# DA q and k projected feature-major, rotary rows exchanged by DMA, attention steps at a priority lifted by 300 places

## The chip, the cores and the metric

One core of a Trainium2 chip runs the program. The metric is the device time of one execution in microseconds (us), as the median of several executions. Five engines take instructions in order, each from its own queue: TensorE (PE, matmuls into PSUM, with weight loads shown apart as PEld), VectorE (DVE), ScalarE (ACT), GpSimd (POOL) and SyncE (SP, which here issues DMAs only). They wait for each other through semaphores.

## The reference, cut to what matters

Two layers of a hybrid mixer run on 512 tokens `x` of width 1024, with 256 context tokens `ctx` that only layer 0 updates. Each layer projects the tokens, runs differential attention (DA, 4 heads), grouped-query attention (GQA, 8 heads on 2 key heads) and a Hyena long convolution, and projects the three outputs back.

```python
h = _rms(x, norm_g[l]) * (1.0 + scale[:, None]) + shift[:, None]
qa, ka, va, ga, qg, kg, vg, gg, uh, gh = _prep(h @ w_in[l], gq_q_g[l], gq_k_g[l])
...
ka_all = jnp.concatenate([ka_c, _rope_2d(ka, tab_da)], axis=1)
va_all = jnp.concatenate([va_c, va], axis=1)
...
y = _mixer_output(_rope_2d(qa, tab_da), ka_all, va_all, ga, _rope_2d(qg, tab_gq), kg_all, vg_all, gg,
                  uh, gh, filt, ...)

def _rope_1d(x, cos, sin):
    x1, x2 = jnp.split(x.astype(jnp.float32), 2, axis=-1)
    return jnp.concatenate([x1 * cos - x2 * sin, x2 * cos + x1 * sin], axis=-1)

def _diff_attend(q, k, v, lam):   # per block of 128 queries
        s = jnp.einsum('bqhcd,bkhcd->bhcqk', qb, k).astype(jnp.float32) * scale
        p = jax.nn.softmax(s, axis=-1)
        a = (p[:, :, 0] - lam * p[:, :, 1]).astype(v.dtype)
        return jnp.einsum('bhqk,bkhe->bqhe', a, v)
```

A DA head has two components c, each with 64 features for q and for k. The rotary step mixes, within a component, feature d with feature d+32 of the same token.

## The kernel before

Every fp32 product is made of three fp32r matmuls (`mm3`, L138 to L140) from a high part and a low part of both factors. The normalized tokens lie in SBUF with features on the partitions (`hT`, as `hx` and `hc`). There are two ways to project. `proj_tok` takes a pair of 128-token blocks as the stationary factor and 256 weight columns as the moving one: tokens come out on the partitions of a PSUM tile `pst` (2 x 8 x 3 = 48 matmuls of 256 columns). `proj_feat` takes 128 weight columns as the stationary factor and all 512 tokens as the moving one: features come out on the partitions of `psf` (8 x 3 = 24 matmuls of 512 columns). Both share two PSUM buffers (`pj`).

The loop over the DA heads works like this before. For each of two pairs of token blocks, `proj_tok` gives q and k of one head token-major. DVE multiplies by the cosine table (L1039) and, with the halves of each component exchanged, by the sine table (L1043, two instructions); POOL adds or subtracts the two (L1046, two instructions). Four PE transposes (L1050) bring the result back into the same PSUM tile, features on partitions. `evac_q` and `evac_k` split it from there into the high and low tiles of pool `up` (20 buffers), with the two components in separate slots. There are 4 heads in each of 2 layers, 8 of these blocks in all; the context's q and k come from `proj_feat` without a rotary step.

Attention is written as generators. `da_att` makes for each group j of 256 queries the scores (`scores_c`, tile S), the softmax (max on DVE, exponential on ACT), the combination of the two components, and then `pv`: for each group of 256 keys four PE transposes of the probabilities (L648, tile T), the split into ph (ACT, L581) and pl (DVE, L582), and the products with V into O (L655 to L658). T and O have one PSUM buffer each. The generators stand in the queue `att`, and each projection calls `att.tock()`, which lets an attention step in at a set pace, so that the steps of one head lie among the projections of the next.

That is the order in which the program is traced. A scheduler then lays each engine's instructions out by priority, which is the place in that traced order, so what stands beside what on an engine is decided when the program is built. SP's queue carries the weight loads (`raw`, `adaw`), the gates (`gl`) and the attention results (`yx`).

Of the kernel before, what the change touches and what calls it, by code (L numbers as in the profile page):

```python
# [3 lines left out]

# [6 lines left out]
F32 = mybir.dt.float32  # L11
F32R = mybir.dt.float32r
AF = mybir.ActivationFunctionType
# [21 lines left out]
class Background:  # L35


    def __init__(self):
        self.queue = deque()
        self.pace = self.due = 1.0  # L40

    def add(self, gen):
        self.queue.append(gen)
# [11 lines left out]
    def tick(self):  # L55
        while self.queue:
            try:
                next(self.queue[0])
                return
            except StopIteration:  # L60
                self.queue.popleft()
# [7 lines left out]
def hybrid_mixer(ctx: ExitStack, tc: tile.TileContext, a, out):  # L69
    nc = tc.nc  # L70
# [49 lines left out]

    bg = Background()
    slow = Background()
    att = Background()
    pre = Background()

    def col(l, c, n=1):
# [407 lines left out]
    def layer(l, hx, hc, late, first):  # L534
# [87 lines left out]
        def scores_c(c, q, kT, klist, i):  # L622
            S = pS.tile([128, 1024], F32, tag="S", name="S")
            m = slice(i * 128, (i + 1) * 128)
            for n, kp in enumerate(klist):
                kh, kl = kT[kp]
                ps = S[:, n * 256:(n + 1) * 256]
                PE.matmul(ps, q[:, c, m], kh[:, c], start=True, stop=False)
                PE.matmul(ps, q[:, c, m], kl[:, c], start=False, stop=True)
            return S  # L630

        def softmax(S, n):
# [359 lines left out]
        for pr in range(2):  # L992
            W = wchunk(l, DA_C[pr]["v"])
            V = {}
            for p in pairs:
                ps = proj_tok(W, p)
                vh = up.tile([128, 2, 256], F32R, tag="u", name="vh")
                vl = up.tile([128, 2, 256], F32R, tag="u", name="vl")
                evac_split(vh, vl, ps)
                V[p] = (vh, vl)  # L1000
            if pr == 0:
                gates(wchunk(l, DA_C[0]["gate"]), 8)
            for hh in range(2):
                head = 2 * pr + hh
                if head == 1:
                    gates(wchunk(l, DA_C[1]["gate"]), 10)
                W = wchunk(l, DA_C[pr]["qk"][hh])
                qT, kT = {}, {}

                def evac_q(p, ps):  # L1010
                    st = up.tile([128, 2, 256], F32R, tag="u", name="qT")
                    ACT.activation(st, ps.unsqueeze(1).to_broadcast([128, 2, 256]), AF.Copy, scale=0.125)
                    for c in range(2):
                        r, o = slice(64 * c, 64 * c + 64), slice(64 - 64 * c, 128 - 64 * c)
                        DVE.scalar_tensor_tensor(out=st[o, c], in0=ps[r], scalar=0.125, in1=st[r, c].bitcast(F32),
                                                 op0=ALU.mult, op1=ALU.subtract)
                    qT[p] = st

                def evac_k(p, ps):
                    kh = up.tile([128, 2, 256], F32R, tag="u", name="kH")  # L1020
                    kl = up.tile([128, 2, 256], F32R, tag="u", name="kL")
                    for c in range(2):
                        POOL.memset(kl[64 - 64 * c:128 - 64 * c, c].bitcast(F32), 0.0)
                    ACT.activation(kh, ps.unsqueeze(1).to_broadcast([128, 2, 256]), AF.Copy)
                    for c in range(2):
                        r = slice(64 * c, 64 * c + 64)
# [3 lines left out]
                    kT[p] = (kh, kl)  # L1030

                for p in (0, 1):
                    ps = proj_tok(W, p)
                    v = ps.rearrange("p t (c d) -> p t c d", d=64)
                    t1 = tp.tile([128, 2, 4, 64], F32, tag="tp", name="t1")
                    t2 = tp.tile([128, 2, 4, 64], F32, tag="tp", name="t2")
                    cb = cosD[:, 2 * p:2 * p + 2].unsqueeze(2).to_broadcast([128, 2, 8, 32])
                    sb = sinD[:, 2 * p:2 * p + 2].unsqueeze(2).to_broadcast([128, 2, 4, 32])
                    DVE.tensor_tensor(out=t1.rearrange("p t c (h d) -> p t (c h) d", d=32),  # L1039
                                      in0=ps.rearrange("p t (c d) -> p t c d", d=32), in1=cb, op=ALU.mult)  # L1040
                    for h in range(2):
                        d, o = slice(32 * h, 32 * h + 32), slice(32 - 32 * h, 64 - 32 * h)
                        DVE.tensor_tensor(out=t2[:, :, :, d], in0=v[:, :, :, o], in1=sb, op=ALU.mult)  # L1043
                    for h in range(2):
                        d = slice(32 * h, 32 * h + 32)
                        POOL.tensor_tensor(out=t1[:, :, :, d], in0=t1[:, :, :, d], in1=t2[:, :, :, d],  # L1046
                                           op=ALU.add if h else ALU.subtract)
                    for qk in range(2):
                        for t in range(2):
                            PE.transpose(ps[:, qk, t * 128:(t + 1) * 128],  # L1050
                                         t1[:, t, 2 * qk:2 * qk + 2].rearrange("p c d -> p (c d)"), ident)
                    evac_q(p, ps[:, 0])
                    evac_k(p, ps[:, 1])
                if full:
                    evac_q(2, proj_feat(W, 0, False))
                evac_k(2, proj_feat(W, 1, False))
# [295 lines left out]
    sinD = cp.tile([128, 4, 32], F32, tag="sinD", name="sinD")  # L1352
    SP.dma_start(sinD, a["sinD"])

    bg.add(f0)
# [6 lines left out]
def _constants():  # L1362
# [19 lines left out]
        return f(np.cos(ang)), f(np.sin(ang))  # L1382

    c["cosG"], c["sinG"] = axial(128)
    c["cosD"], c["sinD"] = axial(64)
# [113 lines left out]
```

## Time and profile before

| | before |
|---|---|
| median of 3 runs | 1597.02 us (1595.21 to 1600.0) |
| profiled execution, its own time | 1593.43 us |
| its span | 1591.7 us |
| granted TensorE clock, share of full | 0.989 |
| PE busy | 1510.1 us, 95% |
| DVE busy | 1127.6 us, 71% |
| ACT busy | 830.9 us, 52% |
| POOL busy | 415.6 us, 26% |

The span runs from the first to the last instruction of the profiled execution. Its own time is 1.7 us longer than the span, and the median of the runs stands 3.6 us above that execution. A matmul's busy time overlaps the next one's, so what a matmul costs on PE is the distance between the starts of two neighbours in the timeline.

### The profile page before, as it was taken

The numbers are of one execution on the slowest core, as the hardware profiler recorded it, in microseconds if no ns is written. First come the engines' busy times: TensorE is split into PE (matmuls) and PEld (weight loads), VectorE is DVE, ScalarE is ACT, GpSimd is POOL, SyncE is SP. The second block draws the span as 40 slices with busy tenths as digits, with TensorE's granted clock in tenths as the row PEclk, the third lists the DMA queues.
The fourth block names the chain that finished last, engine by engine and source line by source line (L and its number), as shares of the span: only waits on it lengthen the run. The fifth ranks groups of instructions, "written<-read, shape, count | busy, mean of one in ns | idle before, by whom it ended". The sixth has DMA issues, their size and how long they took to land.

```text
span 1591.7 us, 29098 instructions
## 1 busy us (share of the span) xinstructions
PE 1510.1 (95%) x11126; PEld 1398.6 (88%) x11126; DVE 1127.6 (71%) x2222; ACT 830.9 (52%) x1673; POOL 415.6 (26%) x451
## 2 busy tenths in 40 slices
PE   5989999999999999998999999999999999898997
PEld 3768889999898989798999977888999998898997
DVE  6789667877776475777755378869877756768755
ACT  5645243555556555566653256334546556656643
POOL 0243443212212141113002114334222222214032
PEclk9999999999999999999999999999999999999999
DMA  9437676423435253315352334674422232115441
GB/s 344 145 111 263 192 222 200 129 76 96 143 102 169 93 159 117 113 48 195 117 179 94 93 108 145 213 229 146 152 75 87 87 97 87 57 51 182 130 133 70
DMA packets 105952, 216.87 MB, mean 136 GB/s; under 512 B 11345, under 2 KB 54291, under 8 KB 105812
## 3 DMA queue, kind: packets, MB, share of 16 engines
q1 hardware_dynamic: 95300, 178.56, 34.9%
q0 software_dynamic: 9936, 35.39, 7.3%
q8 instruction: 88, 1.44, 0.4%
q10 hardware_dynamic: 576, 1.05, 0.2%
q14 instruction: 52, 0.43, 0.1%
HBM read 174.45 MB, written 40.52 MB: 135 GB/s over the span
## 4 chain that ended last, share of the span: by engine, by line
PE 79%; DVE 9%; DMA 4%; issue 3%; ACT 3%; POOL 1%; SPq 0%; POOLq 0%; DVEq 0%; ACTq 0%
PE psf L138 7%; PE psf L139 7%; PE psf L140 7%; PE pst L138 6%; PE pst L140 6%; PE pst L139 6%; PE px L138 4%; PE px L140 4%; PE px L139 4%; PE T L648 4%; PE O L658 2%; PE O L655 2%; PE O L656 2%; PE S L138 2%; PE S L140 2%
## 5 line engine op out<-in xcount | busy, mean ns | idle before, releaser
L138 PE MATMUL psf<-hT,wh 128*128 128x512 f32 (+1 forms) x768 | 267.9, 353 | 8.8 <-DVE cv L687 5.0
L138 PE MATMUL pst<-wh,hT 128*128 128x256 f32 x960 | 273.8, 285 | 0.2
L139 PE MATMUL pst<-wl,hT 128*128 128x256 f32 x960 | 273.7, 285 | 0.0
L140 PE MATMUL pst<-wh,hT 128*128 128x256 f32 x960 | 273.6, 285 | 0.0
L139 PE MATMUL psf<-hT,wh 128*128 128x512 f32 (+1 forms) x768 | 268.4, 350 | 0.0
L140 PE MATMUL psf<-hT,wl 128*128 128x512 f32 (+1 forms) x768 | 268.2, 349 | 0.0
L156 DVE TENSOR_TENSOR wl<-raw,wh 128x1024 fp32r<-128x1024 f32 x136 | 174.6, 1285 | 40.1 <-ACT wh L152 38.7
L152 ACT ACTIVATE wh<-raw 128x1024 fp32r<-128x1024 f32 x136 | 143.5, 1056 | 90.1 <-PE psf L139 34.7
L140 PEld LDWEIGHTS pst<-wh,hT 128*128 128x128 f32 x960 | 183.9, 192 | 1.7 <-issue 1.7
L138 PEld LDWEIGHTS pst<-wh,hT 128*128 128x128 f32 x960 | 184.0, 192 | 1.6 <-issue 1.1
L139 PEld LDWEIGHTS pst<-wl,hT 128*128 128x128 f32 x960 | 183.9, 192 | 0.2
L138 PE MATMUL px<-wh,yT 128*128 128x256 f32 x640 | 181.6, 284 | 1.1 <-DMA yT<-yx 0.6
L140 PE MATMUL px<-wh,yT 128*128 128x256 f32 x640 | 181.6, 284 | 0.2 <-DVE yT L1083 0.2
L139 PE MATMUL px<-wl,yT 128*128 128x256 f32 x640 | 181.5, 284 | 0.0
L637 ACT ACTIVATE P<-S,sa 128x768 f32<-128x768 f32 (+1 forms) x160 | 130.2, 814 | 87.3 <-DVE sa L634 59.1
L138 PEld LDWEIGHTS psf<-hT,wh 128*128 128x128 f32 x768 | 146.3, 191 | 29.0 <-ACT kH L1029 3.2
L140 PEld LDWEIGHTS psf<-hT,wl 128*128 128x128 f32 x768 | 146.5, 191 | 17.9 <-issue 0.8
L139 PEld LDWEIGHTS psf<-hT,wh 128*128 128x128 f32 x768 | 146.9, 191 | 17.3 <-issue 1.2
L634 DVE TENSOR_REDUCE sa<-S 128x1 f32<-128x768 f32 (+1 forms) x160 | 134.6, 841 | 21.8 <-PE S L140 11.9
L582 DVE TENSOR_TENSOR pl<-T,ph 128x512 fp32r<-128x512 f32 x156 | 107.1, 687 | 49.0 <-ACT ph L581 44.2
L581 ACT ACTIVATE ph<-T 128x512 fp32r<-128x512 f32 x156 | 92.7, 594 | 86.5 <-PE T L648 85.6
L138 PEld LDWEIGHTS px<-wh,yT 128*128 128x128 f32 x640 | 122.1, 191 | 2.1 <-ACT pm L1152 0.9
(300 smaller groups left out, 3559.8 us busy)
## 6 DMA issues: line engine op xcount, KB each, us to landing
raw<-in_w_in SPq DMA_DIRECT2D x104, 512.0 KB, 4.1
adaw<-in_ada_w SPq DMA_DIRECT2D x32, 512.0 KB, 4.4
raw<-in_w_out SPq DMA_DIRECT2D x32, 512.0 KB, 3.8
tab<-in_inv POOLq DMA_DIRECT2D x20, 512.0 KB, 4.6
tab<-in_fwd POOLq DMA_DIRECT2D x18, 512.0 KB, 5.1
adaw<-in_ada SPq DMA_DIRECT2D x16, 512.0 KB, 10.7
yT<-yx POOLq DMA_DIRECT2D x16, 512.0 KB, 7.1
gl<-gd SPq DMA_DIRECT2D x60, 128.0 KB, 2.3
```

The costliest lines, as they stand in the source:

```text
L138: i0 = PE.matmul(ps, sh, mh, start=first, stop=False)
L139: PE.matmul(ps, sh, ml, start=False, stop=False)
L140: return i0, PE.matmul(ps, sl, mh, start=False, stop=last)
L152: ACT.activation(hi, src, AF.Copy)
L156: last_lo[0] = e.tensor_tensor(out=lo, in0=src, in1=hi.bitcast(F32), op=ALU.subtract)
L581: ACT.activation(dh, ps, AF.Copy)
L582: return DVE.tensor_tensor(out=dl, in0=ps, in1=dh.bitcast(F32), op=ALU.subtract)
L634: DVE.tensor_reduce(out=nm, in_=S[:, :n], axis=AX.X, op=ALU.max, negate=True)
L637: ACT.activation(P[:, :n], S[:, :n], AF.Exp, bias=nm, accum_out=s)
L648: PE.transpose(T[:, kk, q * 128:(q + 1) * 128], aa[q][:, (2 * i + kk) * 128:(2 * i + kk + 1) * 128], ident)
L655: PE.matmul(O, vh, ph[:, kk], start=(i == 0 and kk == 0), stop=False)
L656: PE.matmul(O, vl, ph[:, kk], start=False, stop=False)
```

## The change

The x tokens' q and k of a DA head are each projected with `proj_feat`. The new `rope_feat` copies the result to SBUF (ACT, L1039 of the changed kernel), exchanges its 32-row blocks through four DMAs on SP (L1042), multiplies the PSUM tile by the cosine table (DVE, L1044), the exchanged copy by the sine table (POOL, L1045), and adds them on DVE (L1046). The splits then read SBUF. `scores_c` has one pair of 512-column matmuls for the x keys. The queue `att` traces its steps at a priority lifted by 300 places. The two tables grow from 64 KB to 256 KB each.

```diff
     def tick(self):
         while self.queue:
             try:
-                next(self.queue[0])
+                with self.tc.high_priority(offset=self.lift) if self.lift else nullcontext():
+                    next(self.queue[0])
                 return
...
-    att = Background()
+    att = Background(tc, 300)
...
-            for n, kp in enumerate(klist):
-                kh, kl = kT[kp]
-                ps = S[:, n * 256:(n + 1) * 256]
-                PE.matmul(ps, q[:, c, m], kh[:, c], start=True, stop=False)
-                PE.matmul(ps, q[:, c, m], kl[:, c], start=False, stop=True)
+            for isx, lo in ([(True, 0), (False, 512)] if len(klist) > 1 else [(False, 0)]):
+                kh, kl = kT[isx]
+                ps = S[:, lo:lo + (L if isx else LC)]
+                PE.matmul(ps, q[:, c, m], kh[c], start=True, stop=False)
+                PE.matmul(ps, q[:, c, m], kl[c], start=False, stop=True)
...
-                def evac_q(p, ps):
+                def evac_q(p, src):
...
-                        DVE.scalar_tensor_tensor(out=st[o, c], in0=ps[r], scalar=0.125, in1=st[r, c].bitcast(F32),
+                        DVE.scalar_tensor_tensor(out=st[o, c], in0=src[r], scalar=0.125, in1=st[r, c].bitcast(F32),
...
-                        DVE.tensor_tensor(out=kl[r, c], in0=ps[r], in1=kh[r, c].bitcast(F32), op=ALU.subtract)
-                    DVE.tensor_copy(kh[64:128, 0], kh[0:64, 0].bitcast(F32))
-                    ACT.activation(kh[0:64, 1], kh[64:128, 1].bitcast(F32), AF.Copy)
...
+                        r, o = slice(64 * c, 64 * c + 64), slice(64 - 64 * c, 128 - 64 * c)
+                        POOL.memset(kl[c][o].bitcast(F32), 0.0)
+                        ACT.activation(kh[c][r], src[r], AF.Copy)
+                        DVE.tensor_tensor(out=kl[c][r], in0=src[r], in1=kh[c][r].bitcast(F32), op=ALU.subtract)
+                        DVE.tensor_copy(kh[c][o], kh[c][r].bitcast(F32))
...
+                def rope_feat(qk):
+                    ps = proj_feat(W, qk, True)
+                    v = tp.tile([128, L], F32, tag="tp", name="dv")
+                    ACT.activation(v, ps, AF.Copy)
+                    w = tp.tile([128, L], F32, tag="tp", name="dw")
+                    for i in range(4):
+                        SP.dma_start(w[32 * i:32 * i + 32], v[32 * (i ^ 1):32 * (i ^ 1) + 32])
+                    f = tp.tile([128, L], F32, tag="tp", name="df")
+                    DVE.tensor_tensor(out=f, in0=ps, in1=cosD, op=ALU.mult)
+                    POOL.tensor_tensor(out=w, in0=w, in1=sinD, op=ALU.mult)
+                    DVE.tensor_tensor(out=f, in0=f, in1=w, op=ALU.add)
+                    return f
+
+                f = rope_feat(0)
+                for p in range(2):
+                    evac_q(p, f[:, p * 256:(p + 1) * 256])
+                evac_k(True, rope_feat(1))
...
-    cosD = cp.tile([128, 4, 32], F32, tag="cosD", name="cosD")
+    cosD = cp.tile([128, L], F32, tag="cosD", name="cosD")
...
-    nc = _bacc.Bacc("TRN2", target_bir_lowering=False, num_devices=1)
+    nc = _bacc.Bacc("TRN2", target_bir_lowering=False, num_devices=1, dynamic_dma_scratch_size=8192)
```

The scheduler's order shows what becomes of it. The first place is PE in layer 0's attention, the same head and key group in both kernels: the transposes of the probabilities (T_7275) and the first product that needs their split (O_7274). Before, five score matmuls and 21 projection matmuls stand between them (7 of those 26 rows here):

```order
L648 MATMUL T_7275<-ident_243,P_7250 128x128
L648 MATMUL T_7275<-ident_243,P_7268 128x128
L629 MATMUL S_7877<-kL_7604,qT_7599 128x256
L628 MATMUL S_7877<-kH_7676,qT_7599 128x256
...
L138 MATMUL pst_8187<-wh_8061,hT_683 128x256
L139 MATMUL pst_8187<-wl_8062,hT_683 128x256
L140 MATMUL pst_8187<-wh_8061,hT_683 128x256
...
L139 MATMUL pst_8260<-wl_8056,hT_592 128x256
L140 MATMUL pst_8260<-wh_8055,hT_592 128x256
L655 MATMUL O_7274<-ph_7280,vv_4592 128x256
```

In the changed kernel one projection matmul stands there, and the next group's transposes follow at once:

```order
L650 MATMUL T_7275<-ident_243,P_7250 128x128
L650 MATMUL T_7275<-ident_243,P_7268 128x128
L142 MATMUL psf_8315<-hT_839,wl_8001 128x256
L657 MATMUL O_7274<-ph_7280,vv_4592 128x256
...
L660 MATMUL O_7274<-pl_7281,vv_4592 128x256 x2
L650 MATMUL T_7290<-ident_243,P_7250 128x128
...
L657 MATMUL O_7274<-ph_7295,vv_4785 128x256
L658 MATMUL O_7274<-ph_7295,vv_4785 128x256
```

So the projection work that stood between a transposition and the product that needs it has moved away at this place.

The second place is PE where a DA head's x tokens are projected. Before, the matmuls have 256 columns, and the transposes of the rotary step stand among those of the next pair:

```order
L140 MATMUL pst_7612<-wh_7472,hT_673 128x256
L138 MATMUL pst_7612<-wh_7472,hT_683 128x256
L1050 MATMUL pst_7539<-ident_243,t1_7588 128x128 x4
L139 MATMUL pst_7612<-wl_7473,hT_683 128x256
L140 MATMUL pst_7612<-wh_7472,hT_683 128x256
```

In the changed kernel q (psf_7539) is followed by k (psf_7583), all with 512 columns and with no transposes:

```order
L141 MATMUL psf_7539<-hT_795,wh_7472 128x512
L142 MATMUL psf_7539<-hT_795,wl_7473 128x512
L140 MATMUL psf_7583<-hT_471,wh_7466 128x512
L141 MATMUL psf_7583<-hT_471,wh_7466 128x512
L142 MATMUL psf_7583<-hT_471,wl_7467 128x512
```

The third place is DVE in the changed kernel, at one of the 16 rotary steps: from the multiplication (L1044) to the addition (L1046, which needs the exchanged and multiplied copy dw_8788), and what is queued behind it. Tiles named `sa` are softmax sums, `pl` the split of the probabilities, `P` the probabilities:

```order
L1044 TENSOR_TENSOR df_8793<-psf_8761,cosD_990 128x512
L976 SCALAR_TENSOR_TENSOR y_7914<-O_7866,sl0_976,gl_7808 128x256
L641 RECIPROCAL sa_8439<-sa_8437 128x1
L966 TENSOR_TENSOR sa_8441<-sa_8439,nl0_973 128x1
L636 TENSOR_REDUCE sa_8450<-S_8445 128x1
L584 TENSOR_TENSOR pl_8069<-T_8063,ph_8068 128x512
L968 SCALAR_TENSOR_TENSOR P_8424<-P_8424,sa_8427,P_8436 128x768
L1046 TENSOR_TENSOR df_8793<-df_8793,dw_8788 128x512
L641 RECIPROCAL sa_8455<-sa_8453 128x1
L636 TENSOR_REDUCE sa_8462<-S_8457 128x1
L584 TENSOR_TENSOR vl_8632<-pst_8582,vh_8631 128x512
L584 TENSOR_TENSOR pl_8084<-T_8078,ph_8083 128x512
```

Here six instructions of attention stand between the two, and attention's next ones wait behind the addition in DVE's queue. SP's queue at this place holds the exchange among the weight loads of the output projection (`raw`) and the gates:

```order
L530 DMA raw_9867<-in_w_out 128x1024
L530 DMA raw_9873<-in_w_out 128x1024
L1042 DMA dw_8788<-dv_8786 32x512 x2
L671 DMA gl_8004<-gd8_171 128x256
L1042 DMA dw_8788<-dv_8786 32x512 x2
L984 DMA yx0_8_127<-y_7914 128x256
L1042 DMA dw_8832<-dv_8830 32x512 x4
```

These eight DMAs are new on SP; the rows around them were there before.

## Rows read from the trace of the kernel before

**Rows 1.** The page: busy time of the engines, and the chain that ended last.

```profile
PE 1510.1 (95%) x11126; PEld 1398.6 (88%) x11126; DVE 1127.6 (71%) x2222; ACT 830.9 (52%) x1673; POOL 415.6 (26%) x451
...
PE 79%; DVE 9%; DMA 4%; issue 3%; ACT 3%; POOL 1%; SPq 0%; POOLq 0%; DVEq 0%; ACTq 0%
```

**Rows 2.** Windows: from:to, length; busy of PE, PEld, DVE, ACT, POOL; clock; DMA.

```profile
300.00:570.00 270.00, 270.00 (x2060) 250.62 (x2059) 188.51 (x403) 152.10 (x330) 63.13 (x65) 1.00 0.37 118
570.00:780.00 210.00, 196.13 (x1518) 182.07 (x1517) 148.94 (x311) 126.59 (x263) 46.38 (x76) 0.98 0.41 131
1300.00:1480.00 180.00, 167.75 (x1305) 160.28 (x1305) 131.24 (x246) 111.38 (x209) 51.00 (x74) 0.99 0.31 100
```

**Rows 3.** Timeline of PE: start, duration; four transposes, then matmuls of 512 columns.

```profile
605.77 0.60 PE L648 MATMUL T<-ident,P 128*128 128x128 f32 x4
606.13 0.48 PE L138 MATMUL psf<-hT,wh 128*128 128x512 f32 x1
606.44 0.39 PE L139 MATMUL psf<-hT,wh 128*128 128x512 f32 x1
...
609.87 0.39 PE L139 MATMUL psf<-hT,wh 128*128 128x512 f32 x1
```

**Rows 4.** Timeline of PE: matmuls of 256 columns, first and last of 16.

```profile
702.14 0.28 PE L140 MATMUL pst<-wh,hT 128*128 128x256 f32 x1
...
703.94 0.28 PE L140 MATMUL pst<-wh,hT 128*128 128x256 f32 x1
```

**Rows 5.** One line's instructions: the rotary step's transposes, min/median/max ns, first and last start.

```profile
L1050 PE MATMUL pst<-ident,t x64: 270/272/327, 567.1 to 1467.1; 128*128 128x128 f32 x64
```

**Rows 6.** Waits of PE, by line and what released it: us, times, longest.

```profile
PE O L655 <- ACT ph L581: 6.2, 6, 3.0
...
PE O L658 <- DVE pl L582: 3.3, 7, 1.2
...
PE psf L138 <- DVE kL L1027: 2.2, 2, 1.2
...
PE pst L1050 <- POOL t L1046: 1.5, 1, 1.5
```

**Rows 7.** Timeline of all engines: one T and its split on ACT.

```profile
718.12 0.60 PE L648 MATMUL T<-ident,P 128*128 128x128 f32 x4
...
718.80 0.58 ACT L581 ACTIVATE ph<-T 128x512 fp32r<-128x512 f32 x1
```

**Rows 8.** Groups of DVE by form: count, busy us, mean ns, idle before and releaser.

```profile
L582 DVE TENSOR_TENSOR pl<-T,ph 128x512 fp32r<-128x512 f32 x156 | 107.1, 687 | 49.0 <-ACT ph L581 44.2 <-PE O L656 3.3
...
L1043 DVE TENSOR_TENSOR t<-pst,sinD 128x256 f32<-128x256 f32 x32 | 12.0, 415 | 0.0
```

**Rows 9.** Groups of ACT by form, the same columns: a copy of 512 columns.

```profile
L574 ACT ACTIVATE gv<-psf 128x512 f32<-128x512 f32 x24 | 14.2, 593 | 20.5 <-PE psf L140 16.6 <-issue 3.8
```

**Rows 10.** Groups of POOL by form: a 512-column product, and the rotary step's half sums.

```profile
L752 POOL TENSOR_TENSOR m<-UW,H 128x512 f32<-128x512 f32 x20 | 26.4, 1338 | 5.1 <-DVE UW L750 2.7 <-DMA H<-sp1x 1.4 <-issue 1.0
L1046 POOL TENSOR_TENSOR t<-t,t 128x256 f32<-128x256 f32 x32 | 24.2, 776 | 55.0 <-DVE t L1043 41.2 <-issue 11.9 <-DVE sa L639 1.8
```

**Rows 11.** DMA issues: count, KB each, median us from issue to landing.

```profile
yx<-tah SPq DMA_DIRECT2D x32, 128.0 KB, 1.8
```

**Rows 12.** Timeline of SP: two DMA issues in one row.

```profile
601.07 0.81 SPq L396 DMA_DIRECT2D adaw<-in_ada_w  x2
```

**Rows 13.** Timeline of DVE near 76 and 90 us: one instruction's form, twice.

```profile
75.94 1.78 DVE L300 TENSOR_TENSOR fw<-fw,bw 128x512 f32<-128x512 f32 x1
...
89.79 0.68 DVE L300 TENSOR_TENSOR fw<-fw,bw 128x512 f32<-128x512 f32 x1
```

**Rows 14.** Timeline of POOL near 76 us.

```profile
75.74 1.43 POOL L294 TENSOR_TENSOR accf<-q,q 128x512 f32<-128x512 f32 x1 [0.81 <-ACT q L292]
```

**Rows 15.** Window of the start-up loads, the columns of rows 2, GB/s last.

```profile
25.00:50.00 25.00, 24.57 (x246) 16.88 (x241) 17.61 (x42) 8.62 (x12) 0.00 (x0) 0.95 0.92 327
```

**Rows 16.** Timeline of ACT: an instruction that waited for a DMA.

```profile
751.05 0.63 ACT L1082 ACTIVATE yT<-yld 128x512 fp32r<-128x512 f32 x1 [1.92 <-DMA yld<-yx]
```

More of the change, by code (lines that the diff above doesn't have):

```diff
@@ L2 @@
 from collections import deque
-from contextlib import ExitStack
+from contextlib import ExitStack, nullcontext
 import numpy as np
@@ L35, with __init__ @@
 class Background:
-    def __init__(self):
+    def __init__(self, tc=None, lift=0):
         self.queue = deque()
         self.pace = self.due = 1.0
+        self.tc, self.lift = tc, lift
     def add(self, gen):
@@ L1008, in layer @@
                 qT, kT = {}, {}
-                def evac_q(p, ps):
+                def evac_q(p, src):
                     st = up.tile([128, 2, 256], F32R, tag="u", name="qT")
-                    ACT.activation(st, ps.unsqueeze(1).to_broadcast([128, 2, 256]), AF.Copy, scale=0.125)
+                    ACT.activation(st, src.unsqueeze(1).to_broadcast([128, 2, 256]), AF.Copy, scale=0.125)
                     for c in range(2):
                         r, o = slice(64 * c, 64 * c + 64), slice(64 - 64 * c, 128 - 64 * c)
-                        DVE.scalar_tensor_tensor(out=st[o, c], in0=ps[r], scalar=0.125, in1=st[r, c].bitcast(F32),
+                        DVE.scalar_tensor_tensor(out=st[o, c], in0=src[r], scalar=0.125, in1=st[r, c].bitcast(F32),
@@ L1016, in evac_q @@
                                                  op0=ALU.mult, op1=ALU.subtract)
                     qT[p] = st
-                def evac_k(p, ps):
-                    kh = up.tile([128, 2, 256], F32R, tag="u", name="kH")
-                    kl = up.tile([128, 2, 256], F32R, tag="u", name="kL")
-                    for c in range(2):
[L1023 to L1026, printed above, removed]
-                        DVE.tensor_tensor(out=kl[r, c], in0=ps[r], in1=kh[r, c].bitcast(F32), op=ALU.subtract)
-                    DVE.tensor_copy(kh[64:128, 0], kh[0:64, 0].bitcast(F32))
-                    ACT.activation(kh[0:64, 1], kh[64:128, 1].bitcast(F32), AF.Copy)
-                    kT[p] = (kh, kl)
@@ L1032, in layer @@
[L1032 to L1053, printed above, removed]
@@ new lines, in evac_k @@
+                def evac_k(isx, src):
+                    n = L if isx else LC
+                    if isx:
+                        kh, kl = [[up.tile([128, n], F32R, tag="u", name=nm) for _ in range(2)] for nm in ("kH", "kL")]
+                    else:
+                        kh, kl = [up.tile([128, 2, n], F32R, tag="u", name=nm) for nm in ("kH", "kL")]
+                        kh, kl = [[v[:, c] for c in range(2)] for v in (kh, kl)]
+                    for c in range(2):
+                        r, o = slice(64 * c, 64 * c + 64), slice(64 - 64 * c, 128 - 64 * c)
[3 more added lines that the diff above has]
+                        DVE.tensor_copy(kh[c][o], kh[c][r].bitcast(F32))
+                    kT[isx] = (kh, kl)
@@ L1054, in layer @@
+                f = rope_feat(0)
+                for p in range(2):
+                    evac_q(p, f[:, p * 256:(p + 1) * 256])
+                evac_k(True, rope_feat(1))
                 if full:
                     evac_q(2, proj_feat(W, 0, False))
-                evac_k(2, proj_feat(W, 1, False))
+                evac_k(False, proj_feat(W, 1, False))
                 att.add(da_att(head, hh, V, qT, kT))
@@ L1348, in hybrid_mixer @@
         subln.append(sg)
-    cosD = cp.tile([128, 4, 32], F32, tag="cosD", name="cosD")
+    cosD = cp.tile([128, L], F32, tag="cosD", name="cosD")
     SP.dma_start(cosD, a["cosD"])
-    sinD = cp.tile([128, 4, 32], F32, tag="sinD", name="sinD")
+    sinD = cp.tile([128, L], F32, tag="sinD", name="sinD")
     SP.dma_start(sinD, a["sinD"])
@@ L1384, in _constants @@
     c["cosG"], c["sinG"] = axial(128)
-    c["cosD"], c["sinD"] = axial(64)
+    cd, sd = [v.transpose(1, 0, 2).reshape(L, 32).T for v in axial(64)]
+    c["cosD"] = np.ascontiguousarray(np.concatenate([cd] * 4))
+    c["sinD"] = np.ascontiguousarray(np.concatenate([-sd, sd] * 2))
     for n in (512, 256):
```

## The prediction

> **What bounds the kernel now.** I read the page first. PE is busy for 1510.1 of 1591.7 us, and the chain that ended last runs 79% over PE, 9% over DVE and 3% over ACT [rows 1]. So most of the time PE waits for nothing but its own queue, and a matmul taken out shortens the end. DVE is no bound by its sum (71%), but it owns the next largest part of that chain.
>
> Then I read windows by stage, since the change lies in attention. From 300 to 570 us (Hyena and GQA) PE is busy for all of the 270 us. The two stretches in which the DA heads are projected and attended, 570 to 780 (layer 0) and 1300 to 1480 us (layer 1), have 13.9 and 12.2 us without PE work [rows 2]. So even there PE sets the pace for 93% of the time, and DVE with 149 of 210 us and 131 of 180 us has room on average, but not always at the right moment.
>
> Last came the waits of PE [rows 6]. Those that the change touches are short: a product waiting for the ACT half of the split probabilities, 6.2 us in 6 waits; for the DVE half, 3.3 us in 7; a rotary transpose waiting for POOL, 1.5 us once; a projection waiting for DVE's k split to free PSUM, 2.2 us in 2.
>
> **What goes: matmuls.** The x projection of a head was 96 matmuls of 256 columns and is 48 of 512. Sixteen starts of the short form are 1.80 us apart, 0.120 each [rows 4]. Sixteen of the long one, from 606.44 to 609.87, are 3.43 us apart, 0.229 each [rows 3]. A head saves 96 x 0.120 - 48 x 0.229 = 0.53 us, and 8 heads 4.3 us. The scores of the x keys, 4 short matmuls against 2 long ones, save 0.022 us each time; there are 2 query groups x 2 blocks x 2 components x 8 heads = 64 of these, 1.4 us. The rotary transposes, 64 of them [rows 5], go altogether. Four cost 0.44 us: 0.36 from the first to the next matmul's start, and 0.08 by which that matmul's successor starts later than the usual 0.229 [rows 3]. Sixteen groups give 7.0 us. That is **12.7 us of PE work**, and with the transpose's wait for POOL [rows 6] **14.2 us**.
>
> The Trainium skill ("TensorE: Matmul & The Clock Gate", section "Back-to-back issue gap") speaks against the first two terms: an isolated warm matmul spaces its successor by N/2.4 + 2.5 ns, so 109 ns for 256 columns and 216 for 512, which would make the projections save about 1.0 us in all, not 4.3, and the 14.2 us about 10; the forecast would then stand some 4 us higher. The rows above are this kernel's own streams and decide it.
>
> **What it puts on other engines.** Per head, DVE loses two cosine products (512 columns, the form and length of the 687 ns split) and four sine products of 415 ns [rows 8], 3.0 us, and gets four 512-column instructions, 2.7 us. The splits change little: the same elements, from SBUF. ACT gets two copies of 512 columns, 2 x 0.593 [rows 9], and loses smaller ones inside the k splits. POOL loses four sums of 776 ns and gets two products of 1338 [rows 10], 0.4 us less. All of it is hidden under PE in the DA stretches, where DVE, ACT and POOL have 61, 83 and 164 us free of 210 [rows 2]. I cost it at nothing; uncovered, ACT's 1.2 us over 8 heads would be 9.5 us.
>
> **What it puts in the way: the exchange.** Before, a rotary step went DVE, POOL, PE. Now DVE's addition waits for: the ACT copy, 0.59 [rows 9]; four DMA issues at 0.4 us each (two in 0.81) [rows 12], 1.6; a landing, for which the nearest row is 1.8 us [rows 11]; and POOL's product, 1.34 [rows 10]. That is 5.3 us from the end of the projection, or 4.6 after DVE has done its own product of 0.69. DVE takes its queue in order. Over the 16 rotary steps I counted in the order what stands between product and addition on DVE: 0, 8, 5, 3, 6, 4, 8, 19, 1, 8, 9, 5, 3, 5, 5 and 15 instructions. DVE's mean instruction takes 1127.6/2222 = 0.51 us [rows 1]. A step is short of cover by 4.6 us less that, so the sixteen miss 29 us together, in which the softmax sums and the splits behind the addition wait too. What this does to the end has two bounds: nothing, if PE has other matmuls ready each time, and 29 us, if every missing microsecond stands in the last chain. The nearest row is DVE's share of that chain, 9%: **+2.6 us**. A gain below nothing is possible as well: PSUM is now free after the cosine product, earlier than after the k split, and the 2.2 us of projections waiting for that [rows 6] could go.
>
> **The lift.** It draws attention's matmuls together. A product with ph can start 1.26 us after its transposes began (718.12 to 718.80, and 0.58) [rows 7]; the transposes themselves fill 0.44, so 0.82 us of other matmuls must stand between; for pl 0.69 more, 1.5 in all. Counted in the order of 156 groups, the first is missing at 13 places before and at 19 after, the second at 10 and 16. The waits of before were 6.2 and 3.3 us [rows 6], 0.48 and 0.33 us for a place. Six more of each cost 2.9 + 2.0 = **+4.9 us**. The bounds: if each of the 12 places lost all that it lacks, 6 x 0.82 + 6 x 0.69 = 9.1 us; if the lift ends the waits of before instead, -9.5 us. I take the rows' price, since PE waits at such places now.
>
> **Smaller terms.** After the change 64 DVE instructions read both factors from SBUF (16 additions, 32 q splits, 16 k splits). One such instruction took 1.78 us at 75.94 beside POOL's own one at 75.74, and 0.68 us at 89.79 without [rows 13, 14]. POOL is busy for 24% of the three stretches [rows 2]; an overlap met at random costs half of the 1.10, so 64 x 0.24 x 0.55 = 8.4 us of DVE, at its 9% **+0.8 us**; bounds nothing and the rival's 6.3 below. The tables add 393 KB at the start, where 327 GB/s move and PE is busy for 24.57 of 25 us [rows 15]: at most 1.2 us, I take **+0.6**. The DMA scratch has no row here; I cost it at nothing.
>
> **Sum.** -14.2 + 2.6 + 4.9 + 0.8 + 0.6 = -5.3 us. The profiled execution of 1593.4 us would be 1588.1. The median of the runs stands 3.6 us above it, so the forecast is **1591.7 us**.
>
> **Rivals.**
>
> 1. *The cut is kept whole and the lift shortens waits.* For it: the waits on ph and pl stand in the profile, and projection matmuls moved out of such places may fill others. Against it: the count of short places rises. Half of those 9.5 us gained: -14.2 + 2.6 - 4.8 + 0.8 + 0.6 = -15.0, **1582 us**.
>
> 2. *The change doesn't do what it says: attention's own chain (max, exponential, combination, T, split, O) sets the length of the DA stretches, and PE idles where the matmuls were.* For it: 26 us idle there, far from the 0 of the stretch before [rows 2]. Against it: 93% busy, which an outside chain would not leave. **1597 us**, and PE idle of some 35 to 40 us in the same stretches.
>
> 3. *Slower: the exchange at the head of DVE's queue.* The addition waits on SP, DMA and POOL, and attention's sums and splits wait behind it; PE, with one T and one O buffer, then stands too. For it: 10 of 16 steps have at most 6 instructions of cover; SP's queue holds weight loads and gates among the exchanges; and the same shape is in the trace on another engine, an ACT instruction that waited 1.92 us for a DMA [rows 16]. Against it: a head's attention starts a head later, so what is blocked is another head's. It turns the sign once more than 7.9 us (5.3 + 2.6) of the 29 reach the end. At half, 14.5 us: **1604 us**.
>
> 4. *Every one of the 64 two-input instructions meets POOL.* 64 x 1.10 x 9% = 6.3 us instead of 0.8, **1597 us**. Against it: POOL's 24%. The Trainium skill ("SBUF — State Buffer", section "Who interferes with whom") has this as a rule: a VectorE instruction with two SBUF inputs contends with a GpSimd instruction that reads SBUF. Rows 13 and 14 agree with it; how often it happens is this kernel's affair.
>
> **How the numbers follow.** A difference under 0.3% (4.8 us) can't be told from none here, so faster means under 1592.2 and slower over 1601.8. The forecast has 0.42, with a range of its own from 1587 to 1596 (the exchange at 0 to 7, or the lift at 0 to 9.1, one at a time); a little more than half of it, 0.25, is faster and 0.17 the same. Rival 1 has 0.20, faster. Rival 2 has 0.12 and rival 4 0.04, the same. Rival 3 has 0.22, slower. Together faster 0.45, same 0.33, slower 0.22. For 8 in 10 the range reaches from 1578 (rival 1 with most of the 9.5 and the 2.2 gained) to 1606 (rival 3 a little past half).
>
> **What would show it.** PE's instructions fall by 576, its busy time by some 12 us less what waits lengthen. Matmuls of `psf` in the rotary step stay 0.229 apart. The waits on ph and pl grow by 3 and 2 us; if they shrink, rival 1 is right. The addition's idle time on DVE, released by POOL, sums to some 29 us; if PE's waits on T, S and O then grow by more than 8 us, rival 3. If PE's idle time in the DA stretches rises by 10 us with no wait on the exchange, rival 2. The q and k splits from SBUF stay near 0.42 us, or rise towards 1.5 by rival 4. I am wrong altogether if the time is decided outside the DA stretches: if the lift moves GQA's or the output projection's matmuls so that a stretch with a full PE, like 300 to 570, gets gaps.

## The result: 1.75% slower

The changed kernel takes 1625.41 us (median of 4 runs, 1622.82 to 1628.52), the kernel before 1597.58 (1595.21 to 1600.0). The ratio is 1.0175, with a 95% interval of 1.015 to 1.02. The forecast was 1591.7 and the range 1578 to 1606; the measured time lies outside, and the sign is wrong.

The page of the changed kernel, its span and the busy time of the engines (before: [rows 1], span 1591.7):

```profile
span 1622.6 us, 28065 instructions
...
PE 1519.1 (94%) x10550; PEld 1377.2 (85%) x10550; DVE 1128.1 (70%) x2198; ACT 835.9 (52%) x1673; POOL 413.3 (25%) x419
```

The 576 matmuls are gone, and yet PE is busy 9.0 us longer. It also idles 103.5 us instead of 81.6. So the 30.9 us of span are 21.9 more idle and 9.0 more busy; set against the 12.7 us that the removed work was worth, PE's remaining matmuls take 21.7 us longer than they did. The mean granted clock tells part of that: 0.980 against 0.989, which over the spans is 32.5 against 17.5 us of lost full-speed time, so up to 15.0 of the 21.7.

The waits of PE in the changed kernel (line, releaser: us, times, longest), to be laid beside [rows 6]:

```profile
PE S L630 <- ACT P L639: 16.9, 15, 2.5
PE O L657 <- ACT ph L583: 9.1, 12, 1.5
...
PE O L657 <- ACT sq L980: 4.8, 4, 1.9
PE T L650 <- DVE pl L584: 4.3, 6, 1.3
...
PE O L660 <- DVE pl L584: 3.4, 5, 1.0
```

The products wait for ph 2.9 us more and for pl 0.1 more: nearly what was forecast for them. But the largest wait is one that the forecast did not count, scores (S) waiting for the exponential (P): 16.9 us, where the trace of before has this:

```profile
PE S L628 <- ACT P L637: 2.9, 6, 0.6
```

The two stretches of [rows 2] now:

```profile
570.00:780.00 210.00, 186.58 (x1186) 159.77 (x1185) 145.81 (x283) 121.81 (x246) 50.73 (x67) 0.95 0.42 133
...
1300.00:1480.00 180.00, 168.91 (x1066) 149.16 (x1065) 126.13 (x214) 107.23 (x194) 41.51 (x51) 1.00 0.35 106
```

PE's idle time in the first has grown from 13.9 to 23.4 us, and its clock has fallen from 0.98 to 0.95; in the second it has fallen a little, from 12.2 to 11.1 us. But the changed kernel runs late, so equal times hold unequal work. Windows from the first to the last DA score of a layer, and from the last score to the end, compare better, though the other matmuls among the scores differ there too. Before, in layer 0, in layer 1 and behind:

```profile
623.40:806.20 182.80, 170.32 (x1350) 161.73 (x1349) 136.74 (x282) 115.51 (x239) 34.51 (x59) 0.98 0.37 118
...
1352.30:1499.80 147.50, 137.66 (x1100) 132.76 (x1099) 112.32 (x210) 95.13 (x178) 35.77 (x55) 0.99 0.30 96
1499.80:1591.70 91.90, 83.25 (x693) 82.76 (x691) 52.86 (x104) 36.29 (x88) 23.67 (x20) 0.98 0.36 115
```

In the changed kernel:

```profile
644.90:826.90 182.00, 161.12 (x1066) 143.72 (x1065) 133.11 (x267) 114.28 (x233) 31.20 (x45) 0.93 0.38 120
...
1384.20:1521.30 137.10, 123.02 (x822) 109.25 (x820) 107.50 (x193) 89.40 (x169) 29.71 (x41) 1.00 0.35 109
1521.30:1622.60 101.30, 87.82 (x697) 86.01 (x696) 53.30 (x104) 37.80 (x91) 23.63 (x20) 0.94 0.31 101
```

Idle time rises by 8.4, 4.2 and 4.8 us. The clock falls in layer 0 (0.98 to 0.93) and at the end (0.98 to 0.94), but not in layer 1. One place in layer 0 shows how PE comes to wait for an exponential. The timeline of all engines from the last matmul of one S (721.73) to the first of the S that needs its buffer (728.28, with its wait and what released it in brackets):

```profile
721.20 2.35 DVE L158 TENSOR_TENSOR wl<-raw,wh 128x1024 fp32r<-128x1024 f32 x2
...
721.73 0.28 PE L631 MATMUL S<-kL,qT 128*128 128x256 f32 x1
...
724.63 0.85 DVE L1017 SCALAR_TENSOR_TENSOR qT<-df,qT 64x256 fp32r<-64x256 f32 x2
...
725.59 0.95 DVE L636 TENSOR_REDUCE sa<-S 128x1 f32<-128x768 f32 x1
...
726.15 0.93 ACT L967 ACTIVATE P<-P,sa 128x768 f32<-128x768 f32 x1
...
727.24 0.90 ACT L639 ACTIVATE P<-S,sa 128x768 f32<-128x768 f32 x1
...
728.28 0.38 PE L630 MATMUL S<-kH,qT 128*128 128x256 f32 x1 [1.99 <-ACT P L639]
```

S has two PSUM buffers, and each is held from its last matmul to the end of its exponential. Here the maximum (L636) starts 3.6 us after the last matmul has ended, behind two weight splits and two q splits on DVE among others, and the exponential 0.7 us after the maximum, behind ACT's scaling of P. The buffer is held for 6.1 us. A third S that comes sooner stops PE, with everything behind it. Around that place (windows, columns as in [rows 2]):

```profile
720.00:730.00 10.00, 6.02 (x36) 4.41 (x35) 9.79 (x18) 7.83 (x16) 1.77 (x3) 1.00 0.41 134
730.00:735.00 5.00, 4.03 (x17) 3.08 (x16) 3.77 (x9) 3.48 (x7) 0.21 (x1) 0.55 0.00 0
```

DVE is full for 10 us (it is not full on average), PE works 6 of them, and in the next 5 us the granted clock is 0.55, near the lower of the two levels (1.2 of 2.4 GHz). So an idle microsecond is paid partly twice here.

### The profile page after: what moved, and what is told of

Read it like the earlier page. It is cut to its first block, busy times and chain, and to the rows that moved or that the text cites. A ratio compares the mean times of both kernels' runs of the same rounds, so it can differ in the third digit from the quotient of the medians.

```text
span 1622.6 us, 28065 instructions
## 1 busy us (share of the span) xinstructions
PE 1519.1 (94%) x10550; PEld 1377.2 (85%) x10550; DVE 1128.1 (70%) x2198; ACT 835.9 (52%) x1673; POOL 413.3 (25%) x419
## 5 line engine op out<-in xcount | busy, mean ns | idle before, releaser
L140 PE MATMUL psf<-hT,wh 128*128 128x512 f32 (+1 forms) x896 | 319.8, 361 | 6.8 <-DVE cv L689 3.8
L141 PE MATMUL psf<-hT,wh 128*128 128x512 f32 (+1 forms) x896 | 319.0, 356 | 0.0
L142 PE MATMUL psf<-hT,wl 128*128 128x512 f32 (+1 forms) x896 | 318.9, 356 | 0.0
L140 PE MATMUL pst<-wh,hT 128*128 128x256 f32 x704 | 200.7, 286 | 2.5 <-DVE t L604 2.4
L141 PE MATMUL pst<-wl,hT 128*128 128x256 f32 x704 | 200.5, 285 | 0.0
L142 PE MATMUL pst<-wh,hT 128*128 128x256 f32 x704 | 200.3, 285 | 0.0
L140 PEld LDWEIGHTS psf<-hT,wh 128*128 128x128 f32 x896 | 170.5, 191 | 34.0 <-issue 2.8
L142 PEld LDWEIGHTS psf<-hT,wl 128*128 128x128 f32 x896 | 171.0, 191 | 21.9
L141 PEld LDWEIGHTS psf<-hT,wh 128*128 128x128 f32 x896 | 171.2, 191 | 20.6 <-issue 0.4
L636 DVE TENSOR_REDUCE sa<-S 128x1 f32<-128x768 f32 (+1 forms) x160 | 134.6, 841 | 25.5 <-PE S L142 17.9
L140 PEld LDWEIGHTS pst<-wh,hT 128*128 128x128 f32 x704 | 134.7, 192 | 6.0 <-issue 2.8
L583 ACT ACTIVATE ph<-T 128x512 fp32r<-128x512 f32 x156 | 92.8, 595 | 90.2 <-PE T L650 89.3
L141 PEld LDWEIGHTS pst<-wl,hT 128*128 128x128 f32 x704 | 134.8, 191 | 1.8 <-issue 1.7
L142 PEld LDWEIGHTS pst<-wh,hT 128*128 128x128 f32 x704 | 134.6, 191 | 0.8 <-issue 0.8
```

Of the source, the lines that this page charges most:

```text
L140: i0 = PE.matmul(ps, sh, mh, start=first, stop=False)
L141: PE.matmul(ps, sh, ml, start=False, stop=False)
L142: return i0, PE.matmul(ps, sl, mh, start=False, stop=last)
L583: ACT.activation(dh, ps, AF.Copy)
L636: DVE.tensor_reduce(out=nm, in_=S[:, :n], axis=AX.X, op=ALU.max, negate=True)
```

## The experiments

All times are medians beside runs of the kernel before on the same chip; the ratio is to these. The counts that later expectations use come from the order of each kernel, as the T to O places did: **S places** are tiles S whose first matmul stands behind less than 4 us of other matmuls (0.229, 0.120 and 0.09 us each) after the last matmul of the S two before; what they lack is summed. The 4 us are a chosen bound. PE's busy and idle time and the clock are those of each profiled execution.

| | median us | ratio (95%) | S places, lack us | PE busy / idle | clock |
|---|---|---|---|---|---|
| before | 1597.58 | 1 | 17, 25 | 1510.1 / 81.6 | 0.989 |
| e12 scores lifted only | 1594.98 | 0.9997 (0.9979 to 1.0015) | 17, 25 | 1512.3 / 82.9 | 0.988 |
| e5 before, lift 1 | 1600.18 | 1.0021 (1.0004 to 1.0037) | 17, 25 | 1516.8 / 84.9 | 0.983 |
| e6 before, lift -100 | 1617.6 | 1.0153 (1.013 to 1.0177) | 30, 43 | 1521.5 / 94.4 | 0.986 |
| e2 before, lift 300 | 1628.24 | 1.0215 (1.0192 to 1.0237) | 26, 39 | 1528.2 / 98.7 | 0.982 |
| e11 all but scores lifted | 1633.23 | 1.0241 (1.0219 to 1.0263) | 37, 65 | 1529.7 / 98.8 | 0.983 |
| e8 no lift, no exchange | 1593.19 | 0.9985 (0.9969 to 1.0001) | 26, 38 | 1504.0 / 83.6 | 0.987 |
| e13 no lift, exchange unwaited | 1600.36 | 1.003 (1.001 to 1.005) | 24, 37 | 1508.8 / 92.4 | 0.983 |
| e1 changed, no lift | 1601.89 | 1.0054 (1.0034 to 1.0074) | 27, 35 | 1511.1 / 92.8 | 0.983 |
| e9 no lift, additions on POOL | 1612.25 | 1.01 (1.0072 to 1.0129) | 27, 39 | 1514.2 / 97.1 | 0.979 |
| e14 changed, lift 1 | 1612.92 | 1.0107 (1.0073 to 1.0142) | 26, 36 | 1517.3 / 99.1 | 0.976 |
| e10 no lift, ACT copies | 1615.42 | 1.013 (1.0111 to 1.0148) | 28, 39 | 1511.8 / 102.8 | 0.980 |
| e7 changed, lift -100 | 1617.98 | 1.0153 (1.0131 to 1.0176) | 38, 58 | 1514.1 / 101.8 | 0.980 |
| e4 changed, lift 100 | 1620.95 | 1.0172 (1.0149 to 1.0195) | 31, 42 | 1515.3 / 105.4 | 0.978 |
| changed (lift 300) | 1625.41 | 1.0175 (1.015 to 1.02) | 33, 47 | 1519.1 / 103.5 | 0.980 |
| e3 lift 300, no exchange | 1642.49 | 1.0308 (1.0286 to 1.033) | 37, 51 | 1527.1 / 111.2 | 0.975 |

**The two halves of the change, e1 and e2.** The changed kernel without lift, and the kernel before with the lift alone:

```diff
 e1, in the changed kernel; e2 the other way round, in the kernel before
-    att = Background(tc, 300)
+    att = Background()
```

> The changed kernel with the queue of attention steps at no lift; projections, exchange and scores as changed. Theory A (the lift draws attention's matmuls together, PE waits on ACT for S and O and then runs at a lower granted clock): the loss of about 28 us goes, and the 14 us cut in PE work shows in part: 1585 to 1598 us, with PE's wait of S on ACT back from 16.9 to about 3 us. Theory B (the exchange at the head of DVE's queue): the loss stays, 1615 to 1630 us. Theory C (any re-laid order of this size is worth some 20 us either way): anything from 1590 to 1625, without the waits following the lift.

> The kernel before with the queue of attention steps lifted by 300 places and nothing else changed. Theory A: slower by 20 to 40 us than before, 1615 to 1640 us, with PE's wait of S on ACT near 17 us and a mean granted clock near 0.98. Theory B: within 10 us of before, 1590 to 1607 us.

The lift alone costs 2.15%, some 34 us; the projections alone cost 0.54%, some 9 us. Together they would make 2.7%, where the changed kernel loses 1.75: each has an order of its own, and the halves don't add up. The engines on the page of e2:

```profile
PE 1528.2 (94%) x11126; PEld 1409.5 (87%) x11126; DVE 1126.4 (69%) x2222; ACT 832.8 (51%) x1673; POOL 415.9 (26%) x451
```

Theory B's first form falls: the lift loses without any exchange. Of theory A the sign holds, but not its number for S: in e2 PE waits 8.6 us for P, not 17, and its loss is 18.1 us of longer busy time and 17.1 of idle time, spread over many waits. E1 misses theory A's range as well: it takes 1601.89 us, and PE's wait of S on P is 8.5 us in it, not 3.

**The exchange under the lift, e3, and a smaller lift, e4.**

```diff
 e3, in the changed kernel
-                    for i in range(4):
-                        SP.dma_start(w[32 * i:32 * i + 32], v[32 * (i ^ 1):32 * (i ^ 1) + 32])
...
-                    POOL.tensor_tensor(out=w, in0=w, in1=sinD, op=ALU.mult)
+                    POOL.tensor_tensor(out=w, in0=v, in1=sinD, op=ALU.mult)
 e4
-    att = Background(tc, 300)
+    att = Background(tc, 100)
```

> The changed kernel without the four exchange DMAs: POOL multiplies the copy itself by the sine table, so the rotary step leaves out the exchange of the halves. Theory A: it stays near 1620 us (1612 to 1628). Theory B: back to 1585 to 1600 us, with DVE's addition no longer idle before it.

> The changed kernel with a lift of 100 places instead of 300. Theory A: between no lift and 300, 1595 to 1615 us, with PE's wait of S on ACT between 3 and 17 us. Theory B: as with 300, 1618 to 1630 us.

Without its DMAs the lifted kernel is slower still, by some 21 us by the ratios and outside both ranges, though DVE's addition waits only 2.1 us in e3. The scheduler had laid another order, with more S places. So taking the exchange out did not bring the loss back, and any comparison of two orders carries such a shift. A lift of 100 costs as much as one of 300 (ratios 1.0172 and 1.0175), which theory A had not said.

**Is it the lift or any new order? e5, e6 and e7.**

```diff
 e5 and e6, in e2's kernel; e7, in the changed kernel, as e6
-    att = Background(tc, 300)
+    att = Background(tc, 1)
...
+    att = Background(tc, -100)
```

> The kernel before with attention steps lifted by one place only. That moves no step earlier by more than a place, but the scheduler lays much of the order out anew. Theory A (what costs is that attention is drawn together): within 6 us of before. Theory C (the order of before is a lucky one, and any re-laying costs): slower by 8 us or more.

> The kernel before with attention steps set back by 100 places, so that more projection matmuls stand between them. Theory A: not slower than before (within 6 us) or faster, with fewer waits of PE on ACT for S and O. Theory C: slower by 8 us or more, as every other order. A third way: the last head's attention ends later and the tail grows; then the end stretch after the last projection is longer while the rest is not.

> The changed kernel with attention set back by 100 places instead of lifted. Theory A: at or below the changed kernel without lift (1602 us): 1585 to 1602. Theory C: between 1600 and 1630 without regard to the lift's sign.

A lift of one place lays a new order and costs 0.2%, so the order of before is not so lucky that every other loses 8 us. But setting attention back by 100 places takes both kernels to 1.5% above before, where drawing it forward by 300 takes them to 2.15 and 1.75%. That fells theory A as I had put it (drawing attention together by a lift). What the costly orders have in common I then looked for in their PE order, and found the S places: 17 in the kernel before and in e5, 26 and 30 in e2 and e6.

**The S places put to the test, e11 and e12.** Both were chosen and expected from the count alone: one lifts everything but the score matmuls, the other nothing else.

```diff
 e11, in e2's kernel, around the score matmuls; e12 with offset=300 and no other lift
+                with tc.high_priority(offset=-300):
```

> The kernel before with attention lifted by 300 places, but the score matmuls (tile S) set back to their own places. In its order a tile S is needed again less than 4 us of matmuls after the last but one at 37 places, which lack 65 us together; 17 places with 25 us before, 26 with 39 under the lift of all steps (1628 us). Theory S (what costs is that scores come before the exponential has freed one of S's two buffers, wherever the lift puts them): slower than the full lift, 1630 to 1655 us. Theory A by T and O alone (short places between transposes and product): 1610 to 1630 us. If it is the early scores that cost, as such: back to within 10 us of before.

> The kernel before with only the score matmuls lifted by 300 places. In its order the places where S is needed again too soon are as before, 17 lacking 25 us. Theory S: within 8 us of before. If it is the early scores that cost, as such: 1615 to 1635 us.

Both came out within theory S's ranges. Lifting the scores alone costs nothing, so it is not early scores that cost. Lifting all but the scores costs as much as lifting all: the ratios, 1.0241 and 1.0215, have intervals that overlap, though the S places rose from 26 to 37. That scores stand too close to one another for two buffers is not shown to be the cost. In e11's order the short places from T to O, counted as in the prediction, have grown too, to 25 for ph and 17 for pl; before has 13 and 10, e12 has 14 and 8. And the wait that the S places stand for does not follow the loss. The waits of e12 (first) and e11:

```profile
PE S L632 <- ACT P L641: 7.0, 8, 1.8
```

```profile
PE S L632 <- ACT P L641: 13.4, 14, 1.9
...
PE O L659 <- DVE y L900: 4.1, 4, 1.6
```

The same wait in e2, which is 2.2% slower than e12, and in e13 (below), which by the ratios is 1.45% faster than the changed kernel with its 16.9 us:

```profile
PE S L630 <- ACT P L639: 8.6, 9, 2.5
```

```profile
PE S L631 <- ACT P L640: 16.9, 12, 5.6
```

In the kernel before the count separates the orders that cost at most 0.2% (17) from those that cost 1.5% and more (26 to 37), but it does not rank the latter: e6 with 30 takes less time than e2 with 26. It is no price list either: orders of the changed projections with 24 to 28 such places took from 1593 to 1615 us.

**Where the projections' gain went, e8, e9, e10, e13 and e14.** All have no lift, except the one place of e14.

```diff
 e8: e3's edit, without lift
 e9
-                    DVE.tensor_tensor(out=f, in0=f, in1=w, op=ALU.add)
+                    POOL.tensor_tensor(out=f, in0=f, in1=w, op=ALU.add)
 e10
-                    ACT.activation(v, ps, AF.Copy)
...
-                        SP.dma_start(w[32 * i:32 * i + 32], v[32 * (i ^ 1):32 * (i ^ 1) + 32])
+                        ACT.activation(w[32 * i:32 * i + 32], ps[32 * (i ^ 1):32 * (i ^ 1) + 32], AF.Copy)
 e13: the DMAs stay, but nothing reads what they bring; u is a tile of its own
+                    POOL.tensor_tensor(out=u, in0=v, in1=sinD, op=ALU.mult)
+                    DVE.tensor_tensor(out=f, in0=f, in1=u, op=ALU.add)
```

> The changed kernel without lift and without the four exchange DMAs: POOL multiplies the copy itself, so the rotary step leaves out the exchange of the halves. If the exchange at the head of DVE's queue is what keeps the changed projections from gaining (about 14 us of PE work less, yet 8 us slower than before): 1580 to 1592 us. If the order decides (Theory C) or attention's own chain: 1596 to 1612 us.

> The changed kernel without lift, with the rotary addition on POOL instead of DVE, so that the wait for the exchange stands in POOL's queue and no softmax stands behind it on DVE; the exchange itself stays. If the exchange costs through DVE's in-order queue (1602 us with it, 1593 without the exchange): 1586 to 1596 us. If it costs through the latency of q and k, or the order alone decides: 1598 to 1610 us.

> The changed kernel without lift, with the exchange made by four ACT copies of 32 rows out of PSUM in place of one copy and four DMAs. It adds three ACT copies of 0.6 us for each of 16 rotary steps and takes SP and the landing out of the chain (5.3 to some 3.7 us). If the exchange costs through the length of that chain: 1590 to 1598 us. If ACT's added 29 us delay exponentials and splits by as much as they save: 1600 to 1612 us.

> The changed kernel without lift, with the four exchange DMAs still made, but into a tile that nothing reads: POOL multiplies the copy itself into a tile of its own, so the rotary step leaves out the exchange, and only the wait for it is gone. If the wait costs (1602 us with it, 1593 without exchange and wait): 1588 to 1597 us, with DVE's idle time before the rotary addition near 2 us instead of 18. If the DMAs themselves cost, by SP's queue or the traffic: 1599 to 1606 us.

> The changed kernel with attention lifted by one place: a newly laid order with as many places where S is needed too soon (26, lacking 36 us) as without lift (27, 35 us). Theory S with the exchange's wait: within 8 us of the changed kernel without lift (1602 us), 1596 to 1610. If the order's luck moves times by more than the counted places say: outside 1590 to 1614.

The waits of DVE and of ACT in the rotary step follow the edits exactly. In e1, DVE's addition waits for POOL, and ACT's split waits for the addition:

```profile
DVE df L1046 <- POOL dw L1045: 18.1, 9, 4.3
...
ACT qT L1014 <- DVE df L1046: 12.8, 5, 5.8
```

In e9 the wait has moved one instruction on, to the splits in ACT's and DVE's queues, and in e10 DVE waits for ACT's copies before its product:

```profile
ACT qT L1014 <- POOL df L1046: 11.2, 3, 6.8
```

```profile
DVE df L1042 <- ACT dw L1040: 24.3, 15, 3.5
```

So moving the latency to another queue does not remove it. In e13 it is gone from DVE:

```profile
DVE df L1048 <- POOL du L1047: 2.4, 4, 0.7
```

and the time is 1600.36 us, hardly less than the 1601.89 of e1 (ratios 1.003 and 1.0054, with intervals that overlap). So 16 us less waiting on DVE brought some 4 us by the ratios. That e8 is 7 us faster than e13 by its ratio is either the DMAs themselves or the order, which these runs don't separate. E14 says how much an order can do: with a count like e1's it is 8 us slower by the ratios, above theory S's range. E8 fell between its two ranges, e9 and e10 above both of theirs, and e13 in the one for the DMAs themselves, so together they don't settle where the gain went. In e13 one wait alone shows this kind of luck: an S of 5.60 us, in part because ACT copies that waited for loads of the output projection stood ahead of the softmax in ACT's queue (two of them, the exponential, and PE):

```profile
756.09 0.63 ACT L1083 ACTIVATE yT<-yld 128x512 fp32r<-128x512 f32 x1 [0.69 <-DMA yld<-yx]
758.01 0.63 ACT L1083 ACTIVATE yT<-yld 128x512 fp32r<-128x512 f32 x1 [1.30 <-DMA yT<-yx]
...
759.68 0.88 ACT L640 ACTIVATE P<-S,sa 128x768 f32<-128x768 f32 x1
...
760.71 0.79 PE L631 MATMUL S<-kH,qT 128*128 128x512 f32 x1 [5.60 <-ACT P L640]
```

No version that computes the whole function is faster than the kernel before.

## Why the prediction was wrong

**The cut of PE work was right, as work.** The matmuls fell by 576, and a 512-column matmul still follows its neighbour by 0.23 us (changed kernel, timeline of PE):

```profile
608.04 0.39 PE L140 MATMUL psf<-hT,wh 128*128 128x512 f32 x1
608.27 0.40 PE L141 MATMUL psf<-hT,wh 128*128 128x512 f32 x1
```

What failed is the sentence on which the sum was built: "a matmul taken out shortens the end". In e1's profiled execution, which is 4 us above its median, the 12.7 us are paid back by 13.7 us of longer busy time and 11.2 of idle time. That is near rival 2, PE idle where the matmuls were, to which I gave 0.12; its objection, that 93% busy leaves no outside chain, took a share of busy time for a proof. Its sign is not met in full: in the two stretches of [rows 2] e1 idles 28.6 us and the changed kernel 34.5, where it said 35 to 40, and that attention's own chain sets the length was not tested. By the count, the removed matmuls had been cover between one S and the next (17 S places before, 27 in e1); that this is what cost is not shown, since e8, which leaves out the exchange, has 26 and is as fast as the kernel before.

**The lift was the step that failed most.** It was priced at +4.9 us with bounds of -9.5 and 9.1, and alone it costs some 34 us (e2); on top of the changed projections 19 by the ratios (1.0175 against 1.0054). The mechanism looked for was of the right kind, too little other work between a PE instruction and what it waits for. But I counted it at the places where PE waited already, T to O, and those two terms (2.9 and 2.0 us) came out at 2.9 and 0.1. The place that had nearly no wait before, S with its two buffers, was left out, and in the changed kernel it is PE's longest wait. It is not the whole price: in e2 it grew by 4.3 us (GQA's scores included) of 17.1 us of idle time, and the rest is spread over many waits. And I priced a wait at its own length alone, while busy time on unchanged work grew by 18.1 us in e2, about as much as the idle time; its clock, 0.982 against 0.989, makes up to 11.8 us of that. The prediction's last sign, time decided outside the DA stretches, came in part: of the 21.9 us more of idle time 12.6 lie between the first and the last DA score of the two layers and 4.8 behind the last one, while the stretch from 300 to 570 us got 1.2 us of gaps.

**The exchange** was sized too short as a chain and too long as a wait. From the projection's end to the addition I had 5.3 us. From the start of ACT's copy to the end of POOL's product the 16 steps took 5.9 to 15.0 us, 6.7 in the median. The first is one of the shortest (ACT's copy starts at 566.45), here DMAs, product and addition:

```profile
567.08 2.48 SPq L1042 DMA_DIRECT2D dw<-dv  x4
```

```profile
571.06 1.29 POOL L1045 TENSOR_TENSOR dw<-dw,sinD 128x512 f32<-128x512 f32 x1 [8.47 <-DMA dw<-dv]
```

```profile
572.39 0.69 DVE L1046 TENSOR_TENSOR df<-df,dw 128x512 f32<-128x512 f32 x1 [4.61 <-POOL dw L1045]
```

The issues were the mis-sized part there, 2.48 us for four instead of 1.6. In the longest step (ACT's copy starts at 758.07) a load of the output projection stood in SP's queue between the first DMA and the others:

```profile
758.69 0.51 SPq L1042 DMA_DIRECT2D dw<-dv  x1
762.39 0.33 SPq L1099 DMA_DIRECT2D yld<-yx  x1
762.76 1.91 SPq L1042 DMA_DIRECT2D dw<-dv  x3
```

DVE waits 16.5 us for the product in the changed kernel and 18.1 in e1, against the 29 counted. Of rival 3 the wait is there, and its sign, more than 8 us more of PE's waits on T, S and O, came too. But it is not shown to be what made the kernel slow: with the lift, e3 has 2.1 us of this wait and is slower still; without it, e13 has 2.4 and is hardly faster than e1.

**The small terms** were small. The 16 additions took 0.843 us on average where their median is 0.692, so contention cost at most 2.4 us of DVE among them. The same sum over the 32 q splits (median 0.420) and the 16 k splits (0.689, of 512 columns) gives 1.4 and 1.1, so 4.9 us for all 64, of 8.4 forecast. The longest two additions stand beside POOL, as this one does:

```profile
1383.53 1.68 DVE L1046 TENSOR_TENSOR df<-df,dw 128x512 f32<-128x512 f32 x1
```

```profile
1383.19 1.47 POOL L887 TENSOR_TENSOR P<-P,sa 128x768 f32<-128x768 f32 x1
```

The Trainium skill ("SBUF — State Buffer", section "Who interferes with whom") has it as a rule that a VectorE instruction with two SBUF inputs contends with a GpSimd instruction that reads SBUF; these two rows agree with it. The larger tables cost nothing that can be seen: attention's first transposes start at 318.55 us, and at 318.64 before.

**What stays open** is the price of an order: that the lift costs is shown by e1 and e2, how it comes to 34 us is not. The S places tell the costly orders of the kernel before from the others, and foretold the ranges of e11 and e12, but e11 has more short places from T to O too, the wait itself does not follow the loss, and orders of nearly equal count differ by 10 us and more. So the single microseconds of e1, e8, e9, e10 and e13 can't be given to one cause.

## What to carry to other kernels

When PE is 95% busy, work taken off it is not yet time saved: PE's busy time is no proof that nothing waits behind it, and the idle time that comes in its place may also bring a lower clock. Look at every PSUM buffer that PE refills, including those that don't wait yet; such a count can warn, but here it gave no price. A lift that moves a whole class of work by hundreds of places is not priced by the waits of today; build the lift alone and measure it. Where a scheduler lays the order, run a neutral edit (a lift of one place) first: it shows by how much a new order moves the time by itself, here some 3 and 8 us.

## What the hardware showed beside this

Four DMA issues of 32 rows from SBUF to SBUF took 2.48 us on SP, 0.62 each (0.58 in the median of all 64), where two loads from memory took 0.81 together [rows 12]. And a stretch of 10 us in which PE worked 6 was followed by 5 us at a granted clock of 0.55.
